# Expert tokens fetched by an indirect DMA in place of a one-hot product, in a two-layer hybrid model

## The chip, the cores and the metric

The kernel runs on one core of one Trainium2 chip. The metric is the time of one execution on the device, in microseconds (us). Engines are named as the profile names them: PE is TensorE's matmul and PEld its weight load, DVE is VectorE, ACT is ScalarE, POOL is GpSimd and SP is SyncE, which here issues the weight DMAs.

## The reference

Two layers work on 512 tokens of 1024 channels: 256 latent tokens and 256 context tokens. Each layer first runs four token mixers and a projection, which the change does not touch. Then it normalises the tokens and sends each to two of 32 experts. The core of that part is:

```python
# hier_moe(h, p): h is (tokens, 1024)
g_sel   = argmax(h @ w_router_g + b_router_g)          # one of 4 groups
top_v, top_i = top_k(e_logits in group g_sel, 2)       # two of 8 experts
weights = softmax(top_v) * g_w
for each expert e and its tokens x_blk:
    hid = silu(x_blk @ w_exp_gate[e]) * (x_blk @ w_exp_up[e])   # 1024 -> 512
    y   = hid @ w_exp_down[e]                                   # 512 -> 1024
out[token] += weight * y
```

In the last layer only the 256 latent tokens are wanted, so its experts work on 256 tokens. All numbers are f32.

## The kernel before, in words

The kernel goes layer by layer. In each layer the mixers come first, then `tail` (L1603), then `moe` (L1642). Tokens lie in tiles of 128: `nt` is 4 in layer 0 and 2 in layer 1.

`tail` runs, for each tile, the projection and `norm2` (L1413). `norm2` makes the normalised row block h2 (128 x 1024, f32), transposes it for the router's logits, and splits it by `split3` into three bf16 pieces, which together hold the f32 value. The pieces lie in `h2p`. Then `route` finds for each token its experts, its weights (`wt3`) and its place among the tokens of each expert (`posm`).

`moe` loops over 16 pairs of experts, each call of `pair` (L1530) doing one pair. Each expert has 64 places, so a pair fills the 128 partitions. The steps of a pair, with the names that the rows use:

- `onehot` on DVE makes oh: for each token and each of the 128 places, whether the token sits there.
- The gather is a product on TensorE: h2p times oh, for 8 blocks of 128 channels, `nt` tiles and 3 pieces. That is 96 bf16 products (pg) in layer 0 and 48 in layer 1. ACT copies the result to xT.
- pT are transposes of oh, which DVE casts to oT. pw are small products that give each place its weight ws.
- pgate and pup: 16 f32 products each, with xT as stationary operand. The two experts use the two halves of TensorE's columns and run beside each other when their products alternate. The trace shows two records for each such instruction.
- hd on ACT and DVE is silu(gate) times up. ph are four transposes of it; ACT copies them to hT.
- pd: 16 products with the down weights. yp is the result scaled by ws, in two f32r pieces (ACT and DVE).
- py: products of oT with yp bring the places back to the tokens. For the first 512 channels DVE multiplies by the layer's gate (tm) and adds to x. For the others ACT copies (ta) and POOL multiplies and adds. There are three ta buffers.

If an expert had more than 64 tokens, `overflow` (L1707) would run further blocks in a loop. In the profiled execution it runs none: the 2304 pg products in the trace are just 16 x 96 and 16 x 48.

The weights come in blocks of 1 MB through SP's queue, 12 for a pair and 192 for a layer. They rotate through slots: `EB` names the number for each layer on either side of SBUF, and with the four that hold the output projection's weights there are 13 in layer 0 and 15 in layer 1. Loading runs ahead as far as slots are free, also during the mixers.

The order of instructions on each engine is made when the program is built: a scheduler of the tile framework orders them by readiness on each engine, so the gather products of the next pair are put in pieces between products of the current one.

Of the kernel before, what the change touches and what calls it, by code (L numbers as in the profile page):

```python
# [2 lines left out]

# [1 line left out]

# [15 lines left out]
D = 1024  # L21
T = 512
EPS = 1e-6
GN_EPS = 64e-5
EB = ((4, 5), (6, 5))
CDEC = math.exp(-0.5)
NEG = -1e30

# [9 lines left out]
C_SLT = C_MG + 128  # L38
C_MA = C_SLT + 128
C_ROPE = C_MA + 256  # L40
C_END = C_ROPE + 128
# [6 lines left out]
def _consts():  # L48
    c = np.zeros((128, C_END), np.float32)
    p = np.arange(128)  # L50
    c[:, C_ID:C_ID + 128] = np.eye(128)
    s = p % 64
    t = np.arange(64)
    c[:, C_MRW:C_MRW + 64] = s[:, None] < t
    c[:, C_MRW + 64:C_MRW + 128] = s[:, None] <= t
    c[:, C_MG:C_MG + 64] = s[:, None] <= t
    c[:, C_MG + 64:C_MG + 128] = s[:, None] >= t
    q = np.arange(128)
    c[:, C_MA:C_MA + 128] = np.where(q[None, :] <= p[:, None], 0.0, NEG)
    c[:, C_MA + 128:C_MA + 256] = np.where(q[None, :] >= p[:, None], 0.0, NEG)  # L60
    c[:, C_BLK:C_BLK + 128] = (p[:, None] // 64) == (p[None, :] // 64)
    tok = np.arange(256, dtype=np.float32)
    inv = np.float32(10000.0) ** (-np.arange(16, dtype=np.float32) / np.float32(16))
    ang = np.concatenate([np.floor(tok / 64)[:, None] * inv, (tok % 64)[:, None] * inv], axis=1)
    ang = ang.astype(np.float32)
    c[:, C_ROPE:C_ROPE + 64] = np.cos(ang).reshape(2, 128, 32).transpose(1, 0, 2).reshape(128, 64)
    c[:, C_ROPE + 64:C_ROPE + 128] = np.sin(ang).reshape(2, 128, 32).transpose(1, 0, 2).reshape(128, 64)

    r = p % 32
    c[:, C_SEL:C_SEL + 12 * L] = r[:, None] == np.arange(12 * L)  # L70
    c[:, C_SLT:C_SLT + 128] = p[:, None] < p[None, :]
# [104 lines left out]
class Net:  # L176
# [1233 lines left out]
            self.tt(xo, xo, tm, OP.add)  # L1410


    def norm2(self, t, x, rw, lo, h2p, wr, lg, pool):  # L1413

        nc = self.nc
        V, G = nc.vector, nc.gpsimd
# [113 lines left out]
    def pair(self, wts, posv, wtv, h2p, x, mb, lo, pool, pooled=(1, 1, 1, 1)):  # L1530

        nc = self.nc
        V, G = nc.vector, nc.gpsimd
        nt = (512 - lo) // 128
        wg, wu, wd = wts
        p = self.onehot(posv, nt, pool, "oh", 2)
        pf = p.rearrange("p t e n -> p t (e n)")
        xT = pool.tile([128, 8, 128], F32, tag="xT", bufs=2, name="xT")
# [12 lines left out]
        oT = pool.tile([128, nt, 128], F32R, tag="oT", bufs=2, name="oT")  # L1551
        V.tensor_copy(oT.rearrange("p t n -> p (t n)"), pT[:, 0:128 * nt])
        pw = self.pc("pw")
        for t in range(nt):
            self.mm(pw[:, 0:6], pf[:, t, :], wtv[:, t], t == 0, t == nt - 1)
        ws = pool.tile([128, 1], F32, tag="ws", bufs=2, name="ws")
        for e in range(2):
            r = slice(64 * e, 64 * e + 64)
            V.tensor_reduce(ws[r], pw[r, 3 * e:3 * e + 3], AX.X, OP.add)
# [25 lines left out]
        for n in range(2):  # L1585
            cs = slice(512 * n, 512 * n + 512)
            for t in range(nt):
                ps = self.pb("py")
                for i in range(2):
                    self.mm(ps, oT[:, t, :], yp[:, i, cs], i == 0, i == 1)  # L1590
                s = (lo // 128 + t) // 2
                xo = x[lo // 128 + t][:, cs]
                if n and pooled[t]:
                    tm = pool.tile([128, 512], F32, tag="ta", bufs=3, name="ta")
                    self.act(tm, ps, AF.Copy)
                    self.tt(tm, tm, mb[s][:, cs], OP.mult, G)
                    self.tt(xo, xo, tm, OP.add, G)
                else:
                    tm = pool.tile([128, 512], F32, tag="tm", bufs=2, name="tm")
                    self.tt(tm, ps, mb[s][:, cs], OP.mult)  # L1600
                    self.tt(xo, xo, tm, OP.add)

    def tail(self, l, lo, acc, rm, w):  # L1603

        nc, io, x = self.nc, self.io, self.x
        nt = (512 - lo) // 128
# [4 lines left out]
        st["h2p"] = h2p = rm.tile([128, 3, nt, D], BF, name="h2p")  # L1611
# [4 lines left out]
        with self.tc.tile_pool(name=f"rt{l}", bufs=1, reuse_waits="tile") as rp:  # L1616
# [12 lines left out]
            lg = self.pc("lg")  # L1629
            for t in range(lo // 128, 4):  # L1630
                self.project(t, w, acc, x, bs, lo, rp)
                self.norm2(t, x, rw, lo, h2p, wr, lg, rp)
# [8 lines left out]

    def moe(self, l, lo, st):  # L1642
        nc, io, x = self.nc, self.io, self.x
        posm, wt3, h2p, mb, plan, base = (st[n] for n in ("posm", "wt3", "h2p", "mb", "plan", "base"))
        banks = self.psum(f"pm{l}", G=2, A=2, B=2, C=2)
        self.bt = "B"
        with self.tc.tile_pool(name=f"ep{l}", bufs=1, reuse_waits="tile") as ep:
            for q in range(16):
                e0 = 2 * q
                wg, wu, wd = [[self.blocks([self.eload(l, 12 * q + 4 * i + 2 * h + e) for h in range(2)])  # L1650
                               for e in range(2)] for i in range(3)]
                posv = [posm[:, :, e0 + e:e0 + e + 1] for e in range(2)]
                wtv = wt3[:, :, e0:e0 + 2, :].rearrange("p t e i -> p t (e i)")
                self.pair((wg, wu, wd), posv, wtv, h2p, x, mb, lo, ep, (1, q < 15, 1, q < 15))
                if q == 0:
                    self.overplan(lo, st["cnt"], plan, base, ep)
            self.overflow(l, x, mb, lo, posm, wt3, plan, base, h2p, ep)
        banks.__exit__(None, None, None)

    def eopen(self, l, side, bufs):  # L1660
# [43 lines left out]
        self.tsc(be, be, 31.0, OP.min)  # L1704
        V.tensor_copy(plan[:, 1:nb + 1], be[0:1])

    def overflow(self, l, x, mb, lo, posm, wt3, plan, base, h2p, pool):  # L1707

        nc, tc, io = self.nc, self.tc, self.io
        V = nc.vector  # L1710
# [4 lines left out]
        with tc.For_i(0, nv, 1) as b:  # L1715
# [16 lines left out]
            self.pair(w, [pe[:, i] for i in range(2)], wv.rearrange("p t e i -> p t (e i)"), h2p, x, mb, lo, pool)  # L1732

    def final(self, x, out, pool):
        nc = self.nc
# [171 lines left out]
```

## Time and profile before

| | us |
|---|---|
| timed runs: median of three (lowest, highest) | 2531.51 (2526.41, 2534.54) |
| profiled execution, its own time | 2508.66 |
| span of the profile | 2506.9 |

| engine | busy us | share of the span |
|---|---|---|
| PE | 2329.0 | 93% |
| PEld | 1397.5 | 56% |
| DVE | 1202.6 | 48% |
| ACT | 670.5 | 27% |
| POOL | 278.0 | 11% |

The mean granted TensorE clock is 0.967 of full speed. The shares are means over stages: the mixers and the expert stages differ, so each stage has to be read by itself. Both windows of the second group of rows below are expert stages: that of layer 0 lies at about 812 to 1393 us from the start of the span, that of layer 1 at about 1990 to 2490 us.

### The profile page before, as it was taken

Reading aid. Unit: us, or ns where it says so; the run is one execution under the profiler, and the core shown is the slowest. Engines: PE = TensorE matmul, PEld = TensorE weight load, DVE = VectorE, ACT = ScalarE, POOL = GpSimd, SP = SyncE. Lnnn points to the kernel's source line nnn. Section 1 sums busy time; section 2 is a strip of 40 time slices with the busy share of each in tenths; the row PEclk is TensorE's granted clock in tenths of the full one; section 3 lists DMA queues with packets and bytes.
Section 4 is the critical chain, followed back from the end, with each engine's and each line's share of the span. In section 5 each row is a group of like instructions: output and inputs, shape, how many; then the busy total and the mean of one; then the engine's idle time right before and its main releaser. Section 6 shows DMA issues by size and latency. Waiting matters only on the chain. (4 is left out here: it accounts for less than half of the span.)

```text
span 2506.9 us, 42482 instructions
## 1 busy us (share of the span) xinstructions
PE 2329.0 (93%) x17303; PEld 1397.5 (56%) x17303; DVE 1202.6 (48%) x3267; ACT 670.5 (27%) x1229; POOL 278.0 (11%) x305
## 2 busy tenths in 40 slices
PE   5999999999998999999999799989899899999996
PEld 4867666677754445444443576767788444333332
DVE  6686666664435333222223678867665432222222
ACT  3254532323212111111111335543323211111111
POOL 0001000000000133132233100100000011111111
PEclk8999999999998999999999899989999899999999
DMA  6343021215723898787887254412227499999993
GB/s 242 121 146 95 29 64 45 73 43 191 263 70 151 339 389 339 309 334 309 350 315 319 74 169 148 131 56 56 90 63 281 154 417 418 401 397 396 396 409 157
DMA packets 143692, 548.23 MB, mean 219 GB/s; under 512 B 35028, under 2 KB 66132, under 8 KB 93060
## 3 DMA queue, kind: packets, MB, share of 16 engines
q1 hardware_dynamic: 138224, 539.51, 56.9%
q10 hardware_dynamic: 5268, 5.94, 0.7%
q8 instruction: 140, 2.29, 0.4%
q14 instruction: 60, 0.49, 0.1%
HBM read 541.78 MB, written 3.60 MB: 218 GB/s over the span
## 5 line engine op out<-in xcount | busy, mean ns | idle before, releaser
L270 PE MATMUL pa<-hh,gs 128*128 128x512 f32 (+2 forms) x1440 | 421.2, 366 | 10.2 <-ACT sg L273 6.1
L270 PEld LDWEIGHTS pa<-hh,gs 128*128 128x128 f32 (+1 forms) x1440 | 252.4, 188 | 69.8 <-issue 15.3
L270 PE MATMUL pd<-w,hT 128*64 128x512 f32 x1024 | 276.6, 599 | 13.1 <-ACT hT L273 12.4
L270 PE MATMUL pa<-hl,gs 128*128 128x512 f32 (+2 forms) x720 | 252.8, 363 | 0.0
L270 PE MATMUL pgate<-w,xT 128*64 128x512 f32 x1024 | 251.3, 596 | 0.0
L270 PE MATMUL pup<-w,xT 128*64 128x512 f32 x1024 | 249.2, 594 | 0.0
L276 POOL TENSOR_TENSOR ta<-ta,mb 128x512 f32<-128x512 f32 x93 | 127.1, 1373 | 1098.2 <-ACT ta L273 1098.2
L270 PEld LDWEIGHTS <-h2p 128*128 128x128 bf16 x2304 | 134.9, 99 | 78.0 <-issue 72.8
L270 PE MATMUL pg<-oh,h2p 128*128 128x128 bf16 x2304 | 163.2, 223 | 5.8 <-DVE nv L1686 4.2
L276 DVE TENSOR_TENSOR gs<-g,gs 128x1024 fp32r<-128x1024 f32 (+1 forms) x106 | 128.1, 1211 | 83.2 <-PE pa L270 56.7
L270 PEld LDWEIGHTS pd<-w,hT 128*64 128x64 f32 x1024 | 81.5, 136 | 146.7 <-issue 124.3
L273 ACT ACTIVATE gs<-g 128x1024 fp32r<-128x1024 f32 (+1 forms) x106 | 110.5, 1045 | 180.7 <-PE pa L270 139.1
L270 PEld LDWEIGHTS pup<-w,xT 128*64 128x64 f32 x1024 | 78.4, 137 | 143.1 <-issue 138.9
L270 PEld LDWEIGHTS pgate<-w,xT 128*64 128x64 f32 x1024 | 74.8, 137 | 139.6 <-issue 129.4
L270 PEld LDWEIGHTS pa<-hl,gs 128*128 128x128 f32 (+1 forms) x720 | 137.1, 190 | 27.3 <-issue 9.1
L270 PE MATMUL py<-yp,oT 128*128 128x512 f32 x384 | 133.1, 441 | 11.2 <-ACT ta L273 5.5
L286 DVE SCALAR_TENSOR_TENSOR hd<-hd,pgate 128x512 f32<-128x512 f32 x32 | 22.0, 688 | 246.7 <-ACT hd L273 246.7
L276 DVE TENSOR_TENSOR hd<-hd,pup 128x512 f32<-128x512 f32 x32 | 22.0, 688 | 218.0 <-PE pup L270 218.0
L276 POOL TENSOR_TENSOR x<-x,ta 128x512 f32<-128x512 f32 x93 | 122.7, 1326 | 4.9
L286 DVE SCALAR_TENSOR_TENSOR yp<-pd,ws,yp 128x512 fp32r<-128x512 f32 x64 | 47.8, 747 | 152.6 <-ACT yp L273 152.6
L273 ACT ACTIVATE yp<-pd,ws 128x512 fp32r<-128x512 f32 x64 | 44.1, 688 | 272.9 <-PE pd L270 272.9
L276 DVE TENSOR_TENSOR tm<-py,mb 128x512 f32<-128x512 f32 x99 | 66.7, 687 | 95.7 <-PE py L270 95.7
(499 smaller groups left out, 3427.1 us busy)
## 6 DMA issues: line engine op xcount, KB each, us to landing
w<-in_w_g SPq DMA_DIRECT2D x128, 1024.0 KB, 7.9
w<-in_w_d SPq DMA_DIRECT2D x128, 1024.0 KB, 10.5
w<-in_w_u SPq DMA_DIRECT2D x128, 1024.0 KB, 8.6
g<-in_w_ada SPq DMA_DIRECT2D x96, 512.0 KB, 4.0
g<-in_w_in_gate SPq DMA_DIRECT2D x64, 512.0 KB, 3.8
g<-in_w_in_rwkv SPq DMA_DIRECT2D x16, 512.0 KB, 3.6
wb<-in_w_branch SPq DMA_DIRECT2D x64, 128.0 KB, 3.1
w<-in_w_out SPq DMA_DIRECT2D x8, 1024.0 KB, 9.3
```

The source lines that it names most:

```text
L270: self.nc.tensor.matmul(out, lhsT, rhs, start=start, stop=stop, skip_group_check=True)
L273: self.nc.scalar.activation(out, in_, f, **kw)
L276: (eng or self.nc.vector).tensor_tensor(out, a, b, op)
L286: self.nc.vector.scalar_tensor_tensor(out, a, s, b, op0=op0, op1=op1)
```

## The change

`norm2` no longer splits h2; SP stores it as f32 rows to DRAM (`h2d`). A new function `seek` makes oh as before, and from it by small products (pw) two numbers per place beside the weight: the token's row number (in two bf16 parts, `tid`) and the count of tokens in the place, 0 or 1. DVE makes an integer index ix, which for an empty place lies beyond the last row. POOL then issues an indirect DMA that fetches the rows of h2d into one of three buffers xg; rows beyond the bound are skipped, and keep what was there (the buffers are set to zero at the start of each layer's experts).

A second new function, `bring`, multiplies xg by the count on DVE, so that empty places become zero. Its scaling is issued behind the product of hd of the preceding pair (`last`). Then TensorE transposes xg in 8 blocks and ACT copies them to xT as before. `pair` keeps the rest. In the program's text, pairs q + 1 and q + 2 are asked for before pair q is computed. `EB` changes, so the slots become 15 in layer 0 and 16 in layer 1. `overflow` uses the same two functions.

```diff
-EB = ((4, 5), (6, 5))
+EB = ((4, 7), (7, 5))
...
+    c[:, C_ROW] = p
...
+        nc.sync.dma_start(h2d[128 * tl:128 * tl + 128], h2)
...
-        self.split3([h2p[:, i, tl, :] for i in range(3)], h2, V)
...
+    def seek(self, posv, wtv, h2d, lo, pool):
+        p = self.onehot(posv, nt, pool, "oh", 3)
+        pf = p.rearrange("p t e n -> p t (e n)")
+        pw = self.pc("pw")
+        for t in range(nt):
+            self.mm(pw[:, 8:11], pf[:, t, :], self.tid[:, t], t == 0, t == nt - 1)
+        for t in range(nt):
+            self.mm(pw[:, 0:6], pf[:, t, :], wtv[:, t], t == 0, t == nt - 1)
...
+        V.tensor_copy(at[:, 0:3], pw[:, 8:11])
+        self.stt(ix, at[:, 0:1], 1024.0, at[:, 1:2], OP.add, OP.add)
...
+        xg = self.xg[self.xi % 3]
+        self.xi += 1
+        nc.gpsimd.indirect_dma_start(xg, None, h2d, bass.IndirectOffsetOnAxis(ap=ix, axis=0),
+                                     bounds_check=128 * nt - 1, oob_is_err=False)
+        return pf, at, ws, xg
...
+    def bring(self, sent, lo, pool, after=None):
+        pf, at, ws, xg = sent
+        with self.tc.issue_after(after) if after is not None else nullcontext():
+            self.tsc(xg, xg, at[:, 2:3], OP.mult)
...
-                for t in range(nt):
-                    for i in range(3):
-                        self.mm(ps[:, 128 * kk:128 * kk + 128], h2p[:, i, t, 128 * k:128 * k + 128], pf[:, t, :],
-                                t == 0 and i == 0, t == nt - 1 and i == 2)
+                nc.tensor.transpose(ps[:, 128 * kk:128 * kk + 128], xg[:, 128 * k:128 * k + 128], self.ident)
...
-        self.tt(hd, hd, pu, OP.mult)
+        last = nc.vector.tensor_tensor(hd, hd, pu, OP.mult).ins
...
+            self.tid = ep.tile([128, nt, 3], BF, name="tid")
...
+            self.xg = [ep.tile([128, D], F32, name=f"xg{i}") for i in range(3)]
+            for xg in self.xg:
+                nc.gpsimd.memset(xg, 0.0)
...
+            sent = seek(0), seek(1)
+            got = self.bring(sent[0], lo, ep)
             for q in range(16):
...
+                sent = sent[1], seek(q + 2)
+                last = self.pair((wg, wu, wd), got, x, mb, lo, ep, (1, q < 15, 1, q < 15))
+                if q < 15:
+                    got = self.bring(sent[0], lo, ep, last)
```

The built orders show where this lands. First TensorE in a steady pair of layer 0, before: between the combine products (py) of one pair and the gate products of the next stand pieces of the gather, each with its stationary operand loaded from h2p.

```order
L270 MATMUL pd<-w,hT 64x512 x7
L270 MATMUL py<-yp,oT 128x512 x4
L270 MATMUL pgate<-w,xT 64x512
L270 MATMUL py<-yp,oT 128x512 x2
L270 LDWEIGHTS h2p
L270 MATMUL pg<-oh,h2p 128x128
```

The same place after the change, from the hidden-state transposes (ph) on: eight transposes of xg stand before pd and between its pieces, and none further on.

```order
L1599 MATMUL ph<-cst,hd 128x128 x4
...
L1571 MATMUL pg<-cst,xg_7792 128x128 x5
L272 MATMUL pd<-w,hT 64x512 x2
L1571 MATMUL pg<-cst,xg_7792 128x128 x2
L272 MATMUL pd<-w,hT 64x512 x7
L1571 MATMUL pg<-cst,xg_7792 128x128
...
L272 MATMUL pd<-w,hT 64x512 x7
L272 MATMUL py<-yp,oT 128x512 x4
L272 MATMUL pgate<-w,xT 64x512
L272 MATMUL py<-yp,oT 128x512 x12
L272 MATMUL pgate<-w,xT 64x512 x15
```

The pieces of gather between py, gate and up are gone; what stays is a cut in pd at two places and one gate product ahead of the last twelve py. Nine pairs of layer 0 read so after the change, the first three have pd, gate and up in one piece each, and the last two before the end lack pw.

On DVE the scaling of xg stands behind the second operation of hd and ahead of the cast of oT and of yp.

```order
L288 SCALAR_TENSOR_TENSOR hd<-hd,pgate 128x512
L1596 TENSOR_TENSOR hd<-hd,pup 128x512
L283 TENSOR_SCALAR xg_7792<-xg_7792,at 128x1024
L1577 CAST oT<-pT 128x512
L288 SCALAR_TENSOR_TENSOR yp<-pd,at,yp 128x512
```

The scaling waits for an indirect DMA, and the cast and yp are queued behind it. On POOL the indirect DMA stands among the operations of ta and x:

```order
L278 TENSOR_TENSOR ta<-ta,mb_7656 128x512
L1555 DMA xg_7791<-h2d_7294,ix 128x1024
L278 TENSOR_TENSOR x_7269<-x_7269,ta 128x512
```

At the start of each layer's experts POOL first has the settings of tid and of the three xg, and then three indirect DMAs, for pairs 0 to 2. From then on the request that is issued beside pair q is that for pair q + 3.

## Rows read from the trace of the kernel before

**Rows 1.** The page: busy share of the DMA engines, in tenths, 40 slices
```profile
DMA  6343021215723898787887254412227499999993
```
**Rows 2.** Windows: us; busy PE, PEld, DVE, ACT, POOL; granted clock; DMA share; GB/s
```profile
812.00:1393.00 581.00, 562.29 (x3505) 253.17 (x3503) 166.24 (x277) 93.92 (x155) 157.96 (x120) 1.00 0.82 324
1990.00:2490.00 500.00, 473.80 (x2561) 192.23 (x2561) 117.83 (x251) 77.65 (x129) 79.09 (x60) 0.99 0.91 372
```
**Rows 3.** The page's groups, gather: busy us, mean ns, idle time before, releaser
```profile
L270 PE MATMUL pg<-oh,h2p 128*128 128x128 bf16 x2304 | 163.2, 223 | 5.8 <-DVE nv L1686 4.2
```
**Rows 4.** PE timeline, steady pair of layer 0: start, us, engine, instruction, idle before
```profile
1088.52 0.66 PE L1572 MATMUL ph<-cst,hd 128*128 128x128 f32 x4 [0.78 <-DVE hd L276]
...
1126.63 0.65 PE L1572 MATMUL ph<-cst,hd 128*128 128x128 f32 x4 [0.78 <-DVE hd L276]
```
**Rows 5.** PE timeline, a late pair of layer 0, without a gather
```profile
1329.32 1.20 PE L270 MATMUL py<-yp,oT 128*128 128x512 f32 x4
...
1351.72 0.66 PE L1572 MATMUL ph<-cst,hd 128*128 128x128 f32 x4 [0.78 <-DVE hd L276]
...
1355.11 7.08 PE L270 MATMUL pd<-w,hT 128*64 128x512 f32 x28
1362.12 1.20 PE L270 MATMUL py<-yp,oT 128*128 128x512 f32 x4
```
**Rows 6.** PE timeline, layer 1: a steady pair, and one without a gather
```profile
2210.32 1.20 PE L270 MATMUL py<-yp,oT 128*128 128x512 f32 x4
...
2242.07 1.19 PE L270 MATMUL py<-yp,oT 128*128 128x512 f32 x4
...
2421.55 0.66 PE L1572 MATMUL ph<-cst,hd 128*128 128x128 f32 x4 [0.78 <-DVE hd L276]
...
2450.91 0.66 PE L1572 MATMUL ph<-cst,hd 128*128 128x128 f32 x4 [0.78 <-DVE hd L276]
```
**Rows 7.** PE timeline, a first pair of layer 0
```profile
867.74 7.09 PE L270 MATMUL pd<-w,hT 128*64 128x512 f32 x32
...
900.18 7.09 PE L270 MATMUL pd<-w,hT 128*64 128x512 f32 x32
```
**Rows 8.** Windows in layer 1: early, and steady
```profile
2015.00:2115.00 100.00, 98.04 (x635) 43.84 (x633) 32.20 (x55) 18.25 (x30) 16.54 (x12) 1.00 1.01 419
2200.00:2400.00 200.00, 190.57 (x1002) 74.70 (x1002) 41.60 (x84) 30.38 (x50) 31.16 (x24) 1.00 0.98 399
```
**Rows 9.** Timeline, PE and DVE: start and ends of both expert stages
```profile
803.86 1.23 DVE L276 TENSOR_TENSOR h2p<-h,h2p 128x1024 bf16<-128x1024 f32 x1 [0.63 <-ACT h2p L273]
...
811.87 7.20 PE L270 MATMUL pg<-oh,h2p 128*128 128x128 bf16 x96 [2.31 <-DVE nv L1686]
...
835.41 7.09 PE L270 MATMUL pd<-w,hT 128*64 128x512 f32 x32
...
1385.86 7.19 PE L270 MATMUL pd<-w,hT 128*64 128x512 f32 x32 [0.69 <-ACT hT L273]
...
1995.40 4.94 PE L270 MATMUL pg<-oh,h2p 128*128 128x128 bf16 x48 [1.84 <-DVE nv L1686]
...
2016.53 7.09 PE L270 MATMUL pd<-w,hT 128*64 128x512 f32 x32
...
2043.82 7.09 PE L270 MATMUL pd<-w,hT 128*64 128x512 f32 x32
...
2481.59 7.19 PE L270 MATMUL pd<-w,hT 128*64 128x512 f32 x32 [0.69 <-ACT hT L273]
```
**Rows 10.** Windows, during the first gather of layer 1
```profile
1996.00:2000.00 4.00, 4.00 (x42) 4.00 (x40) 0.47 (x3) 0.60 (x1) 0.00 (x0) 0.52 0.02 4
```
**Rows 11.** The page: two costly groups (DVE, POOL), and a load's issue to landing
```profile
L276 POOL TENSOR_TENSOR ta<-ta,mb 128x512 f32<-128x512 f32 x93 | 127.1, 1373 | 1098.2 <-ACT ta L273 1098.2
...
L276 DVE TENSOR_TENSOR gs<-g,gs 128x1024 fp32r<-128x1024 f32 (+1 forms) x106 | 128.1, 1211 | 83.2 <-PE pa L270 56.7
...
g<-in_w_ada SPq DMA_DIRECT2D x96, 512.0 KB, 4.0
```

More of the change, by code (lines that the diff above doesn't have):

```diff
@@ L1 @@
 import math
-from contextlib import ExitStack
+from contextlib import ExitStack, nullcontext
 import numpy as np
@@ L1410, in project, with norm2 @@
             self.tt(xo, xo, tm, OP.add)
-    def norm2(self, t, x, rw, lo, h2p, wr, lg, pool):
+    def norm2(self, t, x, rw, lo, h2d, wr, lg, pool):
         nc = self.nc
-        V, G = nc.vector, nc.gpsimd
+        V = nc.vector
         s, tl = t // 2, t - lo // 128
@@ L1528, in onehot @@
         return p
-    def pair(self, wts, posv, wtv, h2p, x, mb, lo, pool, pooled=(1, 1, 1, 1)):
+    def seek(self, posv, wtv, h2d, lo, pool):
         nc = self.nc
-        V, G = nc.vector, nc.gpsimd
+        V = nc.vector
         nt = (512 - lo) // 128
-        wg, wu, wd = wts
-        p = self.onehot(posv, nt, pool, "oh", 2)
+        p = self.onehot(posv, nt, pool, "oh", 3)
         pf = p.rearrange("p t e n -> p t (e n)")
+        pw = self.pc("pw")
[3 more added lines that the diff above has]
+            self.mm(pw[:, 0:6], pf[:, t, :], wtv[:, t], t == 0, t == nt - 1)
+        ix = pool.tile([128, 1], I32, tag="ix", bufs=3, name="ix")
+        at = pool.tile([128, 4], F32, tag="at", bufs=3, name="at")
+        V.tensor_copy(at[:, 0:3], pw[:, 8:11])
+        self.stt(ix, at[:, 0:1], 1024.0, at[:, 1:2], OP.add, OP.add)
+        ws = at[:, 3:4]
+        for e in range(2):
+            r = slice(64 * e, 64 * e + 64)
+            V.tensor_reduce(ws[r], pw[r, 3 * e:3 * e + 3], AX.X, OP.add)
+        xg = self.xg[self.xi % 3]
[4 more added lines that the diff above has]
+    def bring(self, sent, lo, pool, after=None):
+        nc = self.nc
+        nt = (512 - lo) // 128
+        pf, at, ws, xg = sent
+        with self.tc.issue_after(after) if after is not None else nullcontext():
+            self.tsc(xg, xg, at[:, 2:3], OP.mult)
         xT = pool.tile([128, 8, 128], F32, tag="xT", bufs=2, name="xT")
@@ L1551, in pair @@
         oT = pool.tile([128, nt, 128], F32R, tag="oT", bufs=2, name="oT")
[L1552 to L1559, printed above, removed]
+        nc.vector.tensor_copy(oT.rearrange("p t n -> p (t n)"), pT[:, 0:128 * nt])
+        return xT, oT, ws
+    def pair(self, wts, got, x, mb, lo, pool, pooled=(1, 1, 1, 1)):
+        nc = self.nc
+        G = nc.gpsimd
+        nt = (512 - lo) // 128
+        wg, wu, wd = wts
+        xT, oT, ws = got
         pg, pu = self.pa("pgate"), self.pa("pup")
@@ L1601, in pair @@
                     self.tt(xo, xo, tm, OP.add)
+        return last
     def tail(self, l, lo, acc, rm, w):
@@ L1610, in tail @@
         st["cnt"] = cnt = rm.tile([128, 32], F32, name="cnt")
-        st["h2p"] = h2p = rm.tile([128, 3, nt, D], BF, name="h2p")
+        st["h2d"] = h2d = self.dr.tile([128 * nt, D], F32, name=f"h2d{l}")
         nb = 4 * nt
@@ L1631, in tail @@
                 self.project(t, w, acc, x, bs, lo, rp)
-                self.norm2(t, x, rw, lo, h2p, wr, lg, rp)
+                self.norm2(t, x, rw, lo, h2d, wr, lg, rp)
             for s in range(lo // 256, 2):
@@ L1643, in moe @@
         nc, io, x = self.nc, self.io, self.x
-        posm, wt3, h2p, mb, plan, base = (st[n] for n in ("posm", "wt3", "h2p", "mb", "plan", "base"))
+        posm, wt3, h2d, mb, plan, base = (st[n] for n in ("posm", "wt3", "h2d", "mb", "plan", "base"))
         banks = self.psum(f"pm{l}", G=2, A=2, B=2, C=2)
@@ L1647, in moe, with seek @@
         with self.tc.tile_pool(name=f"ep{l}", bufs=1, reuse_waits="tile") as ep:
+            nt = (512 - lo) // 128
+            self.tid = ep.tile([128, nt, 3], BF, name="tid")
+            nc.gpsimd.memset(self.tid[:, :, 2:3], 1.0)
+            for t in range(nt):
+                nc.gpsimd.memset(self.tid[:, t, 1:2], 128.0 * t - 1024.0)
+            nc.vector.tensor_copy(self.tid[:, :, 0:1], self.const(C_ROW, 1, ep)[:, None, :].to_broadcast([128, nt, 1]))
+            self.xg = [ep.tile([128, D], F32, name=f"xg{i}") for i in range(3)]
+            self.xi = 0
+            for xg in self.xg:
+                nc.gpsimd.memset(xg, 0.0)
+            def seek(q):
+                if q > 15:
+                    return None
+                posv = [posm[:, :, 2 * q + e:2 * q + e + 1] for e in range(2)]
+                wtv = wt3[:, :, 2 * q:2 * q + 2, :].rearrange("p t e i -> p t (e i)")
+                return self.seek(posv, wtv, h2d, lo, ep)
+            sent = seek(0), seek(1)
+            got = self.bring(sent[0], lo, ep)
             for q in range(16):
-                e0 = 2 * q
                 wg, wu, wd = [[self.blocks([self.eload(l, 12 * q + 4 * i + 2 * h + e) for h in range(2)])
                                for e in range(2)] for i in range(3)]
-                posv = [posm[:, :, e0 + e:e0 + e + 1] for e in range(2)]
-                wtv = wt3[:, :, e0:e0 + 2, :].rearrange("p t e i -> p t (e i)")
-                self.pair((wg, wu, wd), posv, wtv, h2p, x, mb, lo, ep, (1, q < 15, 1, q < 15))
+                sent = sent[1], seek(q + 2)
+                last = self.pair((wg, wu, wd), got, x, mb, lo, ep, (1, q < 15, 1, q < 15))
+                if q < 15:
+                    got = self.bring(sent[0], lo, ep, last)
                 if q == 0:
                     self.overplan(lo, st["cnt"], plan, base, ep)
-            self.overflow(l, x, mb, lo, posm, wt3, plan, base, h2p, ep)
+            self.overflow(l, x, mb, lo, posm, wt3, plan, base, h2d, ep)
         banks.__exit__(None, None, None)
@@ L1705, in overplan, with overflow @@
         V.tensor_copy(plan[:, 1:nb + 1], be[0:1])
-    def overflow(self, l, x, mb, lo, posm, wt3, plan, base, h2p, pool):
+    def overflow(self, l, x, mb, lo, posm, wt3, plan, base, h2d, pool):
         nc, tc, io = self.nc, self.tc, self.io
@@ L1731, in overflow @@
                 V.tensor_copy(wv[:, :, i, :], wt3[:, :, bass.ds(e, 1), :].rearrange("p t o i -> p t (o i)"))
-            self.pair(w, [pe[:, i] for i in range(2)], wv.rearrange("p t e i -> p t (e i)"), h2p, x, mb, lo, pool)
+            sent = self.seek([pe[:, i] for i in range(2)], wv.rearrange("p t e i -> p t (e i)"), h2d, lo, pool)
+            self.pair(w, self.bring(sent, lo, pool), x, mb, lo, pool)
     def final(self, x, out, pool):
```

3 lines of the change are left out of this document (2 added, 1 removed).

## The prediction

> **What bounds the kernel now.** I read the page's slices first, then stretches by stage, then the costliest groups, then TensorE's timeline through one pair of experts.
>
> The slices show DMA low for most of the first 13, at 7 to 9 tenths in slices 14 to 22, low again to slice 30, and full from slice 33 to 39 [rows 1]. Slices 14 to 22 and 33 to 39 are the two mixture-of-experts (MoE) stages, where the change lies: TensorE is busy 562.29 of 581 us in layer 0 and 473.80 of 500 in layer 1, at a granted clock of 1.00 and 0.99 (the 2.4 GHz level) [rows 2]. DMA's share is 0.82 and 0.91. So TensorE sets the pace, and DMA has 18% left in layer 0 but little in layer 1.
>
> Among TensorE's groups, the gather by products (pg) is 2304 products and 163.2 us [rows 3]. Those go. They are not 163 us on the path, though: many stand where TensorE would wait anyway. Three kinds of pair show this. A steady pair of layer 0 takes 1126.63 - 1088.52 = 38.1 us from one hidden-state transpose (ph) to the next [rows 4]. A late pair, with no gather left to do, takes 1362.12 - 1329.32 = 32.8 us from one combine (py) to the next [rows 5]. So carrying a gather costs 5.3 us, not the 96 products' busy time. In layer 1 a steady pair takes 2242.07 - 2210.32 = 31.75 us and a pair without gather 2450.91 - 2421.55 = 29.36: a difference of 2.4 for 48 products [rows 6]. The first pairs of layer 0, whose gate, up and down products stand unbroken, take 900.18 - 867.74 = 32.4 us with the gather inside [rows 7].
>
> The other floor is the weight stream. Early in layer 1 it runs at 419 GB/s [rows 8]. A pair needs 12 blocks of 1 MB (12.58 MB), which is 30.0 us at that rate. In the steady part of layer 1 the share is 0.98 at 399 GB/s: 31.5 us per pair, next to the 31.75 of TensorE.
>
> **The change, part by part.**
>
> *Gather off TensorE.* The measure for a steady pair is the late pair of before, since its order already has what the changed order keeps: pd cut near its start, so that 28 of its 32 records stand apart (two records to an instruction), and one pgate product ahead of the others. To its 32.8 us come, in layer 0: five transposes of gathered rows ahead of pd, which also wait for the DVE scaling behind hd; two and one more between pieces of pd; four more small pw products; one more cut in pd. Four such transposes (ph) take 0.66 us with their tail [rows 5], so eight take about 1.0 to 1.3. The scaling of 128x1024 on DVE I price by a 128x1024 operation of the trace, 1.21 us [rows 11]. It starts when hd is done, as ph does, and so ends 1.2 us behind ph's start; pd can start 1.35 us behind it, since ph takes 0.66 and the wait for the hT copy 0.69 [rows 9]. So the scaling is hidden and the five transposes, ready just when pd would be, are not: I take +0.6 ahead of pd and +0.9 for the rest: 34.3 us. The bounds are 32.8 (all hidden) and 36.3 (scaling and transposes in full, 1.2 + 1.3, and a second cut's 1.0).
>
> The changed order has three fast pairs (pd, gate and up unbroken), one half broken, nine steady ones, two without pw. Fast pairs lose all pg pieces; the waits that those filled come back, so I take 32.4 - 2.0 = 30.4. The sum is 3 x 30.4 + 34.4 + 9 x 34.3 + 2 x 33.9 = 502.1 us. Before, the fifteen periods run from pd at 835.41 to pd at 1385.86 = 550.4 [rows 9]. Layer 0: -48.
>
> For layer 1 a steady pair is 29.36 + 1.3 = 30.7 (bounds 29.4 and 31.75). The first pairs took 2043.82 - 2016.53 = 27.3 [rows 9] with a gather that filled waits; I take 27.75 for two such, 28.5 for one half broken, ten steady, two without pw 30.3: 451.6 us, against 2481.59 - 2016.53 = 465.1 [rows 9]. Layer 1: -13.5. The smaller figure follows from half the gather, and from TensorE having had less in its way.
>
> *DMA.* A pair now gathers at most 64 rows of 4 KB on the mean in layer 0 (512 tokens, two experts each, over 16 pairs): 0.26 MB, 0.6 us at 419 GB/s; half in layer 1. The floors become 30.7 and 30.3 us per pair, just under 34.3 and 30.7. The stores of normed rows to DRAM (four and two of 512 KB) cost SP four and two places in its queue, ahead of weights that have waited anyway. More weight slots (13 to 15, 15 to 16) let up to 2 MB come during the mixers. No wait of TensorE in rows 4 to 6 ends on a weight, so I count nothing for them; they are what keeps the first three pairs, at 30.4 against 30.7, from running dry.
>
> *The start of each layer's MoE.* This is the side that speaks against the change. Before, the one-hots are followed by 96 products in 7.20 us (48 in 4.94) and then gate [rows 9]. Now: index products, a copy and an addition on DVE, the indirect DMA, the scaling, eight transposes, two copies. DVE also loses the wait for the h2p split in the router (0.63 us, and the operation of 1.23) [rows 9]: -1.9. The indirect DMA has no row before; the nearest is 4.0 us for a 512 KB load from issue to landing [rows 11]; as bounds I take half of it, for half the bytes, and 2.5 times it, 10, for descriptors that a program writes. With 4.0: two one-hots and the tid cast ahead 2.3, products and index 1.3, DMA 4.0, scaling 1.2, transposes and copies 2.7, summing to 11.5 against 8.2 before; less 1.9 it is +1.7 in layer 0 (rounded), and +3 in layer 1, where only 5.0 us of products go. On top comes the clock: in layer 1 it is granted 0.52 during the gather's products [rows 10], so near the lower level (1.2 GHz), and for the stage as a whole 0.99 [rows 2]. TensorE had done little before the gather, and the gather bore the slow start. Now gate's own products stand there. I take 2.5 us for each. The start costs +4.2 and +5.5.
>
> The Trainium skill, page "DMA: Bandwidth & Descriptors", section "Anatomy of one DMA — SWDGE (gpsimd) path", gives such a DMA 2.0 us plus its bytes at 436 GB/s. An estimate by it for 0.26 MB is 2.6 us, 1.4 below the row; by it the sum would be 2.8 us lower. No run here shows it yet.
>
> *Waits added.* On POOL the indirect DMA stands between two additions to x. Behind it are the remaining ta products and additions, and ScalarE waits for those only through three ta buffers. POOL's load is 93 ta products at 1.37 us [rows 11] and as many additions; four of each per pair are about 10.8 of 34 us. So 20 us and more are free for writing descriptors. On DVE the scaling waits for rows that were asked for one pair and some 14 us earlier: about 48 us. That is well over the 10 us bound, so I count nothing for this wait; at landing times over 48 us each pair would lengthen by the excess.
>
> *Sum.* -48.3 - 13.5 + 4.2 + 5.5 = -52. The profiled execution is 2508.66 us (span 2506.9 and 1.8 around it), so 2457. The median of the timed runs is 2531.51, which is 22.9 above the profiled one; the same -52 gives 2480.
>
> **The rivals.**
>
> *DMA becomes the bound.* In its steady part layer 1 has a share of 0.98 at 399 GB/s [rows 8], which may be all it gets with reads, gathers and slot returns mixed; then a pair stays at 31.6 and layer 1 gains only 1 or 2 us, while 4 KB rows take 0.3 us more per pair in layer 0. For it: the share. Against it: 419 GB/s in the stretch before, and no TensorE wait ending on a weight. -48 + 5 - 1.5 + 9.7, plus some 2 of queueing: -33, 2498 us.
>
> *The pair is as short as the work removed says.* Broken products cost only because pieces of gather separated the two experts' halves, and with them gone the steady pair falls to the DMA floor: 15 x 30.7 = 461 and 15 x 30.35 = 455 less the two quick first pairs, 449. -90 - 16 + 10 = -96, 2436 us. Against it: the late pair without gather still takes 32.8, since the cut in pd and the waits on DVE and ScalarE stay.
>
> *Slower: the indirect DMA is slow.* Its place is POOL. If POOL needs more than 23 us for each (34 less 10.8), then ta buffers stay taken, ScalarE and py wait, and each pair lengthens by the excess; if landing takes more than 48 us, the scaling holds DVE, behind which stands the yp operation, and pd's banks. At 30 us for each, a pair is 30 + 10.8 = 40.8 in layer 0, 6.5 over the forecast, and 30 + 5.4 = 35.4 in layer 1, 4.7 over; with 13 requests beside pairs in each layer that is 85 + 61 - 52 = +94: 2625 us. It decides from 26.5 us on (13 x 3 + 13 x 1.2 is 54). For it: descriptors for 128 rows are written by a program, and no row shows its speed. Against it: much slack.
>
> The Trainium skill, page "SBUF — State Buffer", section "SBUF: two separate sides", warns that a DMA issued from GpSimd cannot have its descriptors written while DVE runs an operation that uses two ports. By it every gather would be held by at most the DVE operation that it meets, 1.2 us here, which 48 us cover; only the first gather of each layer would pay, +2.4 us in all. No run here shows it yet.
>
> **How the numbers follow.** My forecast 64% (2466 to 2498 by its own bounds), DMA bound 19%, short pairs 9%, slow indirect DMA 8%. The range goes from 2440 to 2512: it takes in the DMA case, and leaves out most of the short one and the slow one. About 0.3% (7.6 us) is what a measurement can tell from no change. The first three cases are all faster: 92%, of which I give 1 away to a mix that ends near nothing, so faster 0.91, same 0.03, slower 0.06.
>
> **What will show it.** No pg product with h2p, and steady pairs of 34.3 us in layer 0 and 30.7 in layer 1. First gate of layer 0 about 821, and layer 1's pd-to-pd total 452. A DVE scaling with a wait on the DMA would show the lead too short; TensorE waits ending on w, or DMA above 0.97 in layer 0, would show the DMA rival; a granted clock of 0.5 lasting into gate shows the start's price. The forecast is wrong if steady pairs stay above 36.3 or fall to the floor.

## The result and the profile after

The changed kernel takes 2457.36 us (median of four, 2448.8 to 2464.22) against 2533.03 of before (median of four, 2526.41 to 2537.51): a ratio of 0.9724, 95% interval 0.9678 to 0.977. That is 76 us less; 52 were forecast. The median falls on the 2457 of the prediction's sum by luck: that sum started from the profiled execution of before, 2508.66, and the one that starts from the median gave 2480. The profiled execution has a span of 2456.5 us, 50.4 below that of before.

The 50 and the 76 differ because the profiled executions differ in the front part, the mixers, whose instructions stand in nearly the same order in both kernels. A window of both shows the granted clock there (before first; columns as in rows 2):

```profile
300.00:400.00 100.00, 92.81 (x948) 64.12 (x949) 74.25 (x258) 41.79 (x93) 0.12 (x1) 1.00 0.18 49
```

The same stretch after:

```profile
300.00:400.00 100.00, 93.20 (x760) 62.15 (x759) 66.70 (x241) 40.66 (x94) 0.00 (x0) 0.90 0.17 46
```

The clock is granted 1.00 before and 0.90 after. The last router product of layer 0 starts at 801.1 us before and 822.3 after. In the nine profiles of the experiments below it starts at 803 to 812 in four and at 821 to 824 in five, and at 803.3 in the kernel that differs from the changed one by its slots alone. So the 21 us of the front go with the execution and not with the change. The stages are therefore compared one by one, each from its own start in the timeline:

| stage | before | after | difference |
|---|---|---|---|
| last router product to first gate, layer 0 | 18.2 | 20.3 | +2.1 |
| first gate to last combine (py), layer 0 | 581.3 | 524.2 | -57.1 |
| last combine of layer 0 to last router product of layer 1 | 585.4 | 586.1 | +0.7 |
| last router product to first gate, layer 1 | 14.4 | 17.4 | +3.0 |
| first gate to last combine, layer 1 | 492.1 | 470.4 | -21.7 |
| after the last combine | 14.4 | 15.7 | +1.3 |

The sum is -71.7 without the front, close to the 76 of the medians.

A steady pair of layer 0 is now this on TensorE. It answers to rows 4 (start, us, engine, instruction, idle before):

```profile
1149.58 0.65 PE L1599 MATMUL ph<-cst,hd 128*128 128x128 f32 x4 [0.78 <-DVE hd L1596]
...
1150.25 0.76 PE L1571 MATMUL pg<-cst,xg 128*128 128x128 f32 x5
1150.94 1.93 PE L272 MATMUL pd<-w,hT 128*64 128x512 f32 x4
1152.81 0.44 PE L1571 MATMUL pg<-cst,xg 128*128 128x128 f32 x2
1153.17 3.65 PE L272 MATMUL pd<-w,hT 128*64 128x512 f32 x14
1156.75 0.33 PE L1571 MATMUL pg<-cst,xg 128*128 128x128 f32 x1
...
1157.25 3.65 PE L272 MATMUL pd<-w,hT 128*64 128x512 f32 x14
...
1183.19 0.66 PE L1599 MATMUL ph<-cst,hd 128*128 128x128 f32 x4 [0.78 <-DVE hd L1596]
```

From ph to ph it is 33.6 us, against 38.1. pd starts 1.36 us behind ph, no later than before: the five transposes lie in the time in which pd had to wait for hT anyway. In layer 1 a steady pair is 30.1 us against 31.75 [rows 6], and the first pairs of layer 0 are 29.7 against 32.4 [rows 7].

What the new operations cost stands in the groups of the trace after (busy us, mean ns, idle before):

```profile
L1571 PE MATMUL pg<-cst,xg 128*128 128x128 f32 x256 | 47.9, 299 | 8.5 <-DVE xg L283 8.5
L1555 POOL DMA_INDIRECT xg<-h2d,ix x32 | 33.2, 1038 | 23.0 <-DVE at L1552 10.0 <-DVE ix L288 8.3 <-issue 1.7
L288 DVE SCALAR_TENSOR_TENSOR ix<-at 128x1 int32<-128x1 f32 x32 | 29.7, 929 | 0.0
L283 DVE TENSOR_SCALAR xg<-xg,at 128x1024 f32<-128x1024 f32 x32 | 24.0, 749 | 3.6 <-DMA xg<-h2d,ix 3.6
```

and in the list of DMA issues (median us from issue to landing):

```profile
xg<-h2d,ix POOLq DMA_INDIRECT x32, 7.9
```

An indirect DMA takes POOL 1.04 us and lands 7.9 us after its issue. The scaling takes 0.75 us, and only the first one of each layer waits for the DMA (3.6 us in both layers together). Windows of the stage of layer 0 and of the steady part of layer 1 (as rows 2 and 8):

```profile
842.60:1363.00 520.40, 487.25 (x2132) 182.23 (x2132) 190.33 (x303) 92.70 (x156) 171.47 (x133) 1.00 0.90 365
2000.00:2300.00 300.00, 286.20 (x1246) 102.40 (x1242) 86.04 (x170) 48.79 (x81) 68.34 (x54) 1.00 1.01 419
```

In layer 1 the stream is now full, at 419 GB/s against 399 [rows 8], with TensorE still waiting for no weight.

### The profile page after: what moved, and what is told of

Same layout as the page of the kernel before. It is cut to its first block, busy times and chain, and to the rows that moved or that the text cites. A ratio compares the mean times of both kernels' runs of the same rounds, so it can differ in the third digit from the quotient of the medians.

```text
span 2456.5 us, 38840 instructions
## 1 busy us (share of the span) xinstructions
PE 2249.3 (92%) x15351; PEld 1310.5 (53%) x15351; DVE 1234.8 (50%) x3353; ACT 658.3 (27%) x1217; POOL 317.8 (13%) x351
## 5 line engine op out<-in xcount | busy, mean ns | idle before, releaser
L272 PE MATMUL pgate<-w,xT 128*64 128x512 f32 x1024 | 262.5, 602 | 0.0
L272 PE MATMUL py<-yp,oT 128*128 128x512 f32 x384 | 126.9, 433 | 31.2 <-ACT ta L275 22.8
L272 PEld LDWEIGHTS pa<-hl,gs 128*128 128x128 f32 (+1 forms) x720 | 138.8, 193 | 29.5 <-issue 10.6
L272 PEld LDWEIGHTS py<-yp,oT 128*128 128x128 f32 x384 | 61.4, 188 | 121.8 <-ACT ta L275 44.1
L272 PE MATMUL pa<-gs,hh 128*128 128x256 f32 x480 | 107.6, 319 | 2.4 <-DVE gs L278 1.8
L288 DVE SCALAR_TENSOR_TENSOR yp<-pd,at,yp 128x512 fp32r<-128x512 f32 x64 | 47.7, 745 | 122.6 <-ACT yp L275 122.6
L275 ACT ACTIVATE yp<-pd,at 128x512 fp32r<-128x512 f32 x64 | 44.0, 688 | 241.7 <-PE pd L272 241.7
```

Source lines behind the costliest of these rows:

```text
L272: self.nc.tensor.matmul(out, lhsT, rhs, start=start, stop=stop, skip_group_check=True)
L275: self.nc.scalar.activation(out, in_, f, **kw)
L288: self.nc.vector.scalar_tensor_tensor(out, a, s, b, op0=op0, op1=op1)
```

## The experiments

What had to be settled: whether the gain comes from the gather's products having gone (my forecast), from the end of cuts between the two experts' products (a rival of the forecast), from the slots, or from the requests' lead. Ratios are against the kernel before on the same chip.

**Old slots.** The changed kernel with one line undone.

```diff
-EB = ((4, 7), (7, 5))
+EB = ((4, 5), (6, 5))
```

> The changed kernel with the weight slots of before (13 in layer 0, 15 in layer 1). Theory (the gain comes from TensorE's row, the slots only fill the start): the pairs stay at 33.6 us in layer 0 and 30.1 in layer 1, and the whole is 0 to 4 us above the changed kernel, since layer 1's stream, which is busy throughout, starts with one 2.5 us block less. Rival (the slots are a part of the gain): all three blocks come late, 7.5 us or more is lost, and TensorE shows waits on w in the first pairs of a layer.

Measured: 0.9707 (0.9647 to 0.9766), median 2452.43 us, not different from the changed kernel. In layer 0 the third pair is 33.3 us instead of 29.7, since the built order cuts its down products one pair earlier; all others, and all of layer 1, are equal within 0.1 us. No TensorE wait ends on w. The slots are not where the gain comes from.

**The kernel before, uncut.** The gather stays on TensorE, all 2304 products; only the order of the products changes. In the diff `after` is the last down product of the preceding pair.

```diff
+    def mmc(self, *a):
+        with self.tc.issue_after(self.prev) if self.prev is not None else nullcontext():
+            self.prev = self.mm(*a)
...
+                with self.tc.issue_after(after) if after is not None else nullcontext():
+                    for t in range(nt):
+                        for i in range(3):
+                            self.mm(ps[:, 128 * kk:128 * kk + 128], h2p[:, i, t, 128 * k:128 * k + 128], pf[:, t, :],
+                                    t == 0 and i == 0, t == nt - 1 and i == 2)
...
-                    self.mm(ps[r], xT[:, k, r], w[e][k], k == 0, k == 7)
+                    self.mmc(ps[r], xT[:, k, r], w[e][k], k == 0, k == 7)
...
-                    self.mm(ps[64 * e:64 * e + 64], hT[:, 128 * j + 64 * e:128 * j + 64 * e + 64], wd[e][4 * n + j],
+                    self.mmc(ps[64 * e:64 * e + 64], hT[:, 128 * j + 64 * e:128 * j + 64 * e + 64], wd[e][4 * n + j],
```

> The kernel before, with its gather by products and its slots, but the 96 (48) gather products of the next pair issued behind the last down product of the current one, and the gate, up and down products each chained in the order of the program, so that no gather piece cuts them. Theory 1 (the number of gather products is what cost): a steady pair of layer 0 falls by at most 2 us from 38.1, to 36 or more, and the whole gains less than 30 us. Theory 2 (what cost was that pieces of gather cut the products of the two experts apart): a steady pair falls to 33.5 us or less, the level of the changed kernel, layer 1 to 30.1, and the whole gains 50 to 65 us with all 2304 products still there.

Measured: 0.9699 (0.962 to 0.9779), median 2446.89 us: as much as the whole change brings. Its timeline through one pair of layer 0:

```profile
1147.62 0.66 PE L1579 MATMUL ph<-cst,hd 128*128 128x128 f32 x4 [0.82 <-DVE hd L280]
1148.96 7.09 PE L270 MATMUL pd<-w,hT 128*64 128x512 f32 x32 [0.46 <-ACT hT L277]
...
1163.58 2.85 PE L270 MATMUL pg<-oh,h2p 128*128 128x128 bf16 x48
1166.45 7.09 PE L270 MATMUL pgate<-w,xT 128*64 128x512 f32 x32
1173.37 7.04 PE L270 MATMUL pup<-w,xT 128*64 128x512 f32 x32
1181.22 0.65 PE L1579 MATMUL ph<-cst,hd 128*128 128x128 f32 x4 [0.82 <-DVE hd L280]
```

A pair takes 33.6 us with 96 gather products in it, as long as a pair of the changed kernel without them. The same products in the pair of rows 4, before:

```profile
1089.86 1.93 PE L270 MATMUL pd<-w,hT 128*64 128x512 f32 x4 [0.46 <-ACT hT L273]
...
1091.91 3.65 PE L270 MATMUL pd<-w,hT 128*64 128x512 f32 x14
...
1096.04 3.65 PE L270 MATMUL pd<-w,hT 128*64 128x512 f32 x14
...
1100.76 1.07 PE L270 MATMUL pgate<-w,xT 128*64 128x512 f32 x2
...
1107.64 7.08 PE L270 MATMUL pgate<-w,xT 128*64 128x512 f32 x30
...
1114.81 1.07 PE L270 MATMUL pup<-w,xT 128*64 128x512 f32 x2
...
1118.77 7.08 PE L270 MATMUL pup<-w,xT 128*64 128x512 f32 x30
```

Down, gate and up take 25.5 us in seven pieces there and 21.2 in three here. These 4.3 us are nearly all of the 4.5 between the two pairs (38.1 and 33.6), so it is the cuts that cost. First gate to last combine is 535.0 and 460.2 us, against 581.3 and 492.1 before: -46.3 and -31.9, together -78.2, where the change has -57.1 and -21.7, together -78.8. In layer 1 a pair takes 28.6 us, less than the changed kernel's 30.1. In layer 0 the first three pairs, which were unbroken before too, rise from 32.4 us to 33.5: there pieces of the gather had stood in the waits ahead of ph and pd. Theory 2 holds, and its 65 us were too few; the number of products alone did not cost the 4.5 us that the change won per pair.

**No scaling.** The line of the scaling is taken out; empty places keep rows of an earlier pair, and their weight is zero.

```diff
-        with self.tc.issue_after(after) if after is not None else nullcontext():
-            self.tsc(xg, xg, at[:, 2:3], OP.mult)
```

> The changed kernel without the scaling of xg by the count on DVE; empty places then keep rows of an earlier pair, which their weight of zero takes out at yp. Theory (the scaling is hidden): pairs within 0.3 us of the changed kernel in sum, unless the built order cuts products elsewhere; it puts the transposes between the first and the other up products, which costs about 1 us per pair, so 0 to +15 us. Rival (the wait of the transposes on the scaling is on the path): each pair 0.7 us shorter, 20 us in all.

Measured: 1.026 (1.0194 to 1.0326), median 2597.09 us, slower than the kernel before, and neither theory said so. The timeline of layer 1:

```profile
2286.44 0.48 PE L1569 MATMUL pg<-cst,xg 128*128 128x128 f32 x1 [4.87 <-DMA xg<-h2d,ix]
2286.84 1.97 PE L272 MATMUL pup<-w,xT 128*64 128x512 f32 x2
2288.74 1.76 PE L1569 MATMUL pg<-cst,xg 128*128 128x128 f32 x7
...
2324.95 0.47 PE L1569 MATMUL pg<-cst,xg 128*128 128x128 f32 x1 [4.76 <-DMA xg<-h2d,ix]
```

and POOL's request:

```profile
2316.73 1.03 POOL L1555 DMA_INDIRECT xg<-h2d,ix  x1
```

The rows asked for at 2316.73 are wanted by TensorE at 2320 and there at 2324.95. Without the scaling nothing ties the transposes to the preceding pair's hd, and the scheduler put them where it held the rows to be there: behind gate of the very pair in which they are asked for. They stand 8 us behind their request, where the scaling of the changed kernel stands 46 us behind it (1103.45 to 1149.45), so over a pair earlier. Each pair waits 4.8 us for the DMA, and the products behind the wait run at a lower clock: two records of up take 1.97 us, where gate's two take 1.07 in the same pair. The granted clock is 0.53 from 2286 to 2291 us, and 0.93 over 2100 to 2500. So the scaling's place does a work that its cost doesn't show: it holds the transposes back.

**The unbroken order, without and with scaling.** To the changed kernel come the chains of the run above, the transposes of xg and the small products of the next request behind the last down product. The second run keeps the scaling.

```diff
-                    self.mm(ps[64 * e:64 * e + 64], hT[:, 128 * j + 64 * e:128 * j + 64 * e + 64], wd[e][4 * n + j],
+                    self.mmc(ps[64 * e:64 * e + 64], hT[:, 128 * j + 64 * e:128 * j + 64 * e + 64], wd[e][4 * n + j],
...
+                with self.tc.issue_after(after[1]) if after is not None else nullcontext():
                     nc.tensor.transpose(ps[:, 128 * kk:128 * kk + 128], xg[:, 128 * k:128 * k + 128], self.ident)
...
-                    got = self.bring(sent[0], lo, ep, last)
+                    got = self.bring(sent[1], lo, ep, last)
+                    sent = sent[1], seek(q + 2, last[1])
```

> The changed kernel without the scaling, and with gate, up and down products chained in program order, the transposes of xg and the small products for the next request behind the last down product. If the cuts in down and gate are what keeps a pair of layer 0 at 33.6 us: 30.6 or so, where the weight stream (12 blocks of 2.5 us and the rows, 30.65) becomes the limit, 35 to 40 us less than the changed kernel in all, with nothing gained in layer 1, whose DMA is busy throughout. If the waits on DVE and ScalarE keep it there: 32.5 or more and less than 15 us.

> The unbroken order with the scaling of xg on DVE kept, behind hd of the preceding pair as in the changed kernel. If the scaling costs nothing where the transposes stand behind the down products: within 5 us of the same kernel without it (2422 us), pairs of 31.0 us in layer 0. If it holds DVE ahead of oT and yp: 0.75 us more per pair of layer 0, 11 us.

Measured: 0.9588 (0.953 to 0.9647), 2422.32 us, without the scaling; 0.959 (0.9535 to 0.9644), 2416.43 us, with it. Both intervals lie below that of the changed kernel, and the scaling costs nothing that shows: layer 0 is 462.1 us from the first ph to the last in either. One pair of the run with scaling:

```profile
1150.64 0.66 PE L1606 MATMUL ph<-cst,hd 128*128 128x128 f32 x4 [0.78 <-DVE hd L1603]
1151.98 7.09 PE L272 MATMUL pd<-w,hT 128*64 128x512 f32 x32 [0.46 <-ACT hT L279]
1181.60 0.66 PE L1606 MATMUL ph<-cst,hd 128*128 128x128 f32 x4 [0.78 <-DVE hd L1603]
```

31.0 us per pair of layer 0. Of the 2.6 us below the changed kernel, 2.1 are the two cuts in pd (1.93 + 3.65 + 3.65 against 7.09); the rest is that transposes and small products no longer stand between pieces of pd. One gate product stays ahead of the last py in this run too (1.07 us), so this cut is in both. The 2.6 us below the uncut kernel of before, whose gate is in one piece, are what the gather's products cost net of that cut; without it they might cost about 1 us more, by an estimate from the 1.07 + 7.08 against 7.09 of gate above. In layer 1 pairs are 26.7 to 27.5 us at first and then 28.3 to 33.0. The waits of TensorE there (sum, times, longest):

```profile
PE pup L272 <- DMA w<-in_w_u: 15.0, 7, 2.4
```

Now TensorE does wait for weights: the blocks loaded ahead are used up, and the stream sets the end. So in layer 1 taking the gather off TensorE wins nothing over putting it in order: from first gate to last combine it is 466.3 us here, and 460.2 in the uncut kernel of before, with the stream at 419 GB/s in both.

**A third of the stream left out.** As the run without scaling, and up uses the gate weights.

> The unbroken order without scaling, but the up products use the gate weights, so that a third of the weight blocks is not loaded (the up weights are left out of the computation, save a few blocks loaded ahead and unread). Theory (layer 1 is bound by the stream there, layer 0 by TensorE): layer 1's pairs all become 26.7 to 27.5 us, without waits on w; layer 0 stays within 0.5 us of its 30.5 to 31.0. Rival (DMA sets layer 0 too): layer 0's pairs fall by 1 us or more.

Measured in one execution (2384.6 us): layer 1's pairs are 26.7 us but for the last (27.4), with no wait on w, and layer 0's 30.5. So TensorE's own length of a pair is 26.7 in layer 1, and the stream holds it at about 30 where the order is unbroken. In layer 0 no wait of TensorE ends on w in any of the unbroken kernels, so TensorE is the bound, but barely: by an estimate from 419 GB/s the stream would take 30.0 and the rows 0.6. Gate is built in other pieces in this run, so its 30.5 against 31.0 does not show the stream's part.

**One cut, odd and even.** In the unbroken order the eight transposes are put behind the fifth, or the fourth, of the 16 down products, and chained there.

```diff
+                    if nxt is not None and (n, 2 * j + e) == (0, CUT):      # CUT = 5 or 4
+                        self.got = self.bring(nxt, lo, pool, 1)
```

> The unbroken order without scaling, but the eight transposes of xg placed behind the fifth of the 16 down products, so that each expert has 3 and 2 products ahead of the cut and 5 and 6 behind it. If products of the two experts run beside each other only inside a stretch, and a stretch lasts as long as its fuller expert (0.857 us for each of 3 + 6 products): the down products take 7.7 + 0.3 us busy in all, against 7.1 in one piece, 0.9 us longer. If a cut costs by its mere presence, the same as an even cut in the next run.

> As the run with an odd cut (fifth product, down products 2.79 + 5.36 = 8.15 us busy in two stretches, against 7.09 in one), but the eight transposes stand behind the fourth of the 16 down products, so that each expert has two products ahead of the cut and six behind it. If a stretch lasts as long as its fuller expert: 1.93 + 5.36 = 7.3 us in two stretches, 0.9 less than the odd cut. If the cut itself costs: 8.1 us as there.

Odd, then even (timeline of layer 0, two records to a product):

```profile
1208.17 2.79 PE L273 MATMUL pd<-w,hT 128*64 128x512 f32 x10 [0.46 <-ACT hT L280]
1210.89 1.09 PE L1576 MATMUL pg<-cst,xg 128*128 128x128 f32 x8
1211.91 5.36 PE L273 MATMUL pd<-w,hT 128*64 128x512 f32 x22
```

```profile
1207.70 1.94 PE L273 MATMUL pd<-w,hT 128*64 128x512 f32 x8 [0.46 <-ACT hT L280]
1209.57 1.09 PE L1576 MATMUL pg<-cst,xg 128*128 128x128 f32 x8
1210.59 5.37 PE L273 MATMUL pd<-w,hT 128*64 128x512 f32 x24
```

8.15 us against 7.31, where one piece takes 7.09. The eleven products behind the odd cut last as long as the twelve behind the even one: a stretch lasts as long as its fuller expert. The cut as such costs 0.2 us, an odd one 0.85 more. In layer 1 this shows in the pair, 29.5 us against 28.6 in the early ones. In layer 0 it does not, 31.5 against 31.7: gate is built in other pieces in the two kernels, and in the even one py waits for ta and tm (0.75 and 0.32 us a pair). The two ran once each on different chips, 2432.66 and 2447.87 us, and these totals settle nothing.

**One pair ahead.** The changed kernel asks for the next pair's rows instead of those of the pair after.

```diff
-                sent = sent[1], seek(q + 2)
+                sent = seek(q + 1)
```

> The changed kernel with one edit: at the program's step for pair q the rows of pair q + 1 are asked for instead of those of q + 2, so each request stands one pair later. The indirect DMA took 8.1 us to land under load, and the scaling that waits for it stands behind hd, some 14 us after the request. Theory (8 us of lead suffice): pairs stay at 33.6 and 30.1, the total within 4 us of the changed kernel. Rival (two pairs ahead are needed): DVE shows waits on the DMA, and pairs grow by those.

Measured: 0.9778 (0.9734 to 0.9823), median 2468.17 us, an interval that overlaps that of the changed kernel. In the profile layer 1 is as there, but layer 0 is 506.3 us from first to last ph, 14 more than in the changed kernel. Where DVE waits, in its timeline:

```profile
887.31 0.69 DVE L1596 TENSOR_TENSOR hd<-hd,pup 128x512 f32<-128x512 f32 x1 [2.32 <-PE pup L272]
892.59 0.75 DVE L283 TENSOR_SCALAR xg<-xg,at 128x1024 f32<-128x1024 f32 x1 [4.59 <-DMA xg<-h2d,ix]
...
926.07 0.75 DVE L283 TENSOR_SCALAR xg<-xg,at 128x1024 f32<-128x1024 f32 x1 [2.17 <-DMA xg<-h2d,ix]
...
959.53 0.75 DVE L283 TENSOR_SCALAR xg<-xg,at 128x1024 f32<-128x1024 f32 x1 [2.03 <-DMA xg<-h2d,ix]
```

and POOL's requests:

```profile
884.18 1.04 POOL L1555 DMA_INDIRECT xg<-h2d,ix  x1 [0.15 <-DVE base L278]
917.49 1.03 POOL L1555 DMA_INDIRECT xg<-h2d,ix  x1
...
967.09 1.12 POOL L1555 DMA_INDIRECT xg<-h2d,ix  x1 [12.31 <-DVE ix L288]
```

The requests for these three pairs (the third at 951.09) come 4 to 6 us ahead of the end of hd, the first of them behind DVE's plan for the overflow, and the landing takes 8. The three waits are 8.8 us. The rest of the 14 is TensorE behind them: pd takes 8.05 and 8.59 us after the first two waits in place of 7.09, at a granted clock of 0.83 and 0.82. The request at 967.09 comes 28 us ahead of the scaling that uses it, and from there on no pair waits. My theory held for layer 1 and most pairs of layer 0 and missed the first ones: the second pair ahead is needed there only, and is worth 14 us in this profile.

## Why the prediction was right, and where its sizes were off

The direction, the range and the main terms held: 2457 lies in 2440 to 2512. The gain was put too low, 52 us where the medians give 76 and the stages 71.7.

*Gather off TensorE.* From the first pd to the last, -48.3 and -13.5 us were forecast in the two layers. Measured are 492.2 us against 550.4 and 442.6 against 465.1, -58 and -22.5. This is the mis-sized term. I took 34.3 us for a steady pair of layer 0 (33.6 measured), 30.7 in layer 1 (30.1), and 30.4 for the fast ones (29.7). The 0.6 ahead of pd was wrong: the five transposes are hidden, since scaling and transposes together end when hT is copied (1.36 us behind ph, against 1.34 before). The other 0.9 for rows and cuts measured 0.8.

*Why the gain is there.* I read rows 4 and 5 as the price of carrying a gather, 5.3 us. The uncut kernel of before shows that most of it was not the products but where they stood: uncut, the gather costs 2.6 us a pair net of the gate cut (33.6 against 31.0), and the order costs 4.5 (38.1 against 33.6), of which the cuts are 4.3. The rival "as short as the work removed says" named the cuts and then expected that they would go; they did not, the changed order kept two in pd and one in gate. Those in pd alone cost 2.1 of the 2.6 us between 33.6 and 31.0: its three stretches are 1.93 + 3.65 + 3.65 = 9.2 us, against 7.09 in one. So the forecast was near the size for a reason that was half the wrong one: the late pair of before, from which it was worked out, lacked both the products and some of the cuts, and could not tell one from the other.

*The first pairs' start.* Forecast were +4.2 and +5.5: +1.7 and +3 for the steps up to the first gate, and 2.5 each for the clock behind it. (The terms of the sum as written, 11.5 - 8.2 - 1.9, make +1.4.) The steps measured +2.1 and +3.0. The clock's part was put too high: from the first gate to the first ph it is 16.1 us in layer 0 and 15.4 in layer 1, against 14.8 in both before, so +1.3 and +0.6. In layer 0 the clock is granted 0.50 from 834.0 to 842.5 and 0.74 from there to 848:

```profile
834.00:842.50 8.50, 3.36 (x36) 2.72 (x36) 4.57 (x22) 0.60 (x1) 3.18 (x3) 0.50 0.37 103
842.50:848.00 5.50, 5.50 (x21) 1.83 (x22) 0.00 (x0) 0.60 (x1) 0.00 (x0) 0.74 0.01 4
```

The mechanism was right, and its price was half of what I took or less. The first request is issued at 835.70 and the scaling starts at 839.88, 4.2 us later, near the 4.0 of the row that I took:

```profile
835.70 1.20 POOL L1555 DMA_INDIRECT xg<-h2d,ix  x1 [9.96 <-DVE at L1552]
839.88 0.75 DVE L283 TENSOR_SCALAR xg<-xg,at 128x1024 f32<-128x1024 f32 x1 [1.70 <-DMA xg<-h2d,ix]
```

The Trainium skill, page "DMA: Bandwidth & Descriptors", section "Anatomy of one DMA — SWDGE (gpsimd) path", makes it 2.6 us by an estimate from its 2.0 plus bytes. The trace does not agree: 4.2 us at a DMA share of 0.37 (the first of the windows above) and 7.9 as the median beside the weight stream.

*DMA as a floor per pair.* That was wrong in form. Pairs of 26.7 us stand in layer 1 of the unbroken kernels, and of 27.1 to 27.4 in the changed one, where I put a floor at 30.3: blocks loaded ahead pay the difference until they are used up. The stream is a floor for the stage, and TensorE waits for it only in the unbroken kernels of the change, late in layer 1.

*The slow indirect DMA.* POOL needs 1.04 us for one, not 26, and the lead, 46 us in a steady pair of layer 0, covers 8. But the place from which it decides was real: with the transposes over a pair earlier (no scaling) the same DMA made the kernel slower than before.

*The Trainium skill's warning,* on the page "SBUF — State Buffer", section "SBUF: two separate sides", that GpSimd cannot write descriptors beside a two-port operation of DVE, shows no price here: all 32 requests lie between 0.99 and 1.2 us of POOL. But DVE runs nothing beside 23 of them, so the case hardly tests it.

*The sum against the medians.* -71.7 by stages; the other four to the 76 of the medians are within their intervals. What stays open is why the front's clock differs by execution: the windows show that it does, and nothing here shows why.

## What to carry to other kernels

When a group of products goes, ask what its pieces did to their neighbours: here their place between the products of two experts cost more than they did themselves, and a rule of order won as much as the change. Compare a pair with and a pair without the work only where the order around them is the same. And when an operation is taken out, ask what its wait held back: the scaling cost nothing, and taking it out alone cost some 135 us (0.054 of 2525).

## What was not expected of the hardware

DVE's index operation on 128 x 1 numbers takes 0.16 us at the start of layer 0, with POOL idle, and 1.23 beside POOL's additions (mean 0.93 over 32):

```profile
834.66 0.16 DVE L288 SCALAR_TENSOR_TENSOR ix<-at 128x1 int32<-128x1 f32 x1
```

```profile
1134.11 1.60 POOL L278 TENSOR_TENSOR x<-x,ta 128x512 f32<-128x512 f32 x1
```

```profile
1134.50 1.23 DVE L288 SCALAR_TENSOR_TENSOR ix<-at 128x1 int32<-128x1 f32 x1
```

It ends at 1135.73, when POOL's addition ends (1135.71). Of the 32, 24 meet an addition or a product of POOL, and each ends within 0.03 us of it; the other eight take 0.15 or 0.16 us. So a tiny operation of DVE can wait out a POOL operation of over a microsecond. The Trainium skill, page "SBUF — State Buffer", section "SBUF: two separate sides", calls the port pair that DVE and GpSimd share an exclusive lock; these rows agree with that. That a landing takes twice as long beside the stream (7.9 against 4.2 us) matters only where the lead is short.
